# Strassen matmul with tanh: cast blocks of the third column, later stores, another order of transfers

## The chip, the cores and the metric

One core of one Trainium2 chip. The metric is the device time of one launch in microseconds (us), the median of three runs. A profile of one further execution goes with it. The engines are TensorE (PE; its weight loads are shown as PEld), VectorE (DVE), ScalarE (ACT), GpSimd (POOL) and SyncE (SP). Transfers are issued from POOL's queue (in the profile q0, software_dynamic) and from SP's (q1, hardware_dynamic); a transfer that changes the number type is always issued from POOL.

## The reference

```python
m, k, n = 4096, 4096, 4096        # a: (m, k), b: (k, n), bias: (n,), all float32
return np.tanh(np.matmul(a, b) + bias)
```

## The kernel before

The output is made in four columns of 1024 (c = 0 to 3), and in each column in pairs of row blocks, 256 rows each. A pair of one column is one level of Strassen's scheme (Winograd's form) with seven products m1 to m7, in 16-bit floats. `a11` to `a22` are the four quarters of a pair's rows of A, `b11` to `b22` those of the column's B, `s1`, `s2`, `s5`, `s6`, `s7` sums of A's quarters, `d1`, `d3`, `d4`, `e6`, `e7` sums of B's. B's operands stay in SBUF for the column, each in four blocks (`blk` 0 to 3, 512 KB in 16 bits).

The work is a list of 61 **items**, numbered n; the prediction speaks of items by these numbers. An item has a column, one pair, or two pairs for half of the inner dimension. Time is laid out by hand in **slots**, seven for an item; item n has its products at slot 7n + position, and a product of 16 matmuls fills about one slot:

```python
PRODUCTS = {
    0: ("m2", "s2", "b11"),
    2: ("m5", "s5", "b22"),
    4: ("m3", "a11", "d3"),
    5: ("m1", "s1", "d1"),
    6: ("m4", "a22", "d4"),
    8: ("m6", "s6", "e6"),
    10: ("m7", "s7", "e7"),
}
```

So at slot 177 stands m5 of item 25, at 179 m3 of 25, at 182 m2 of 26, at 184 m5 of 26, at 200 m3 of 28. `at_slot(slot, f, ...)` hangs any other work ahead of the products of that slot; each engine takes its instructions in the order in which they are written, and so does each transfer queue.

Items by column: 0 to 12 in column 0, 13 to 28 in column 1, 29 to 44 in column 2, 45 to 60 in column 3. The last two items of a column (11 and 12, 27 and 28, 43 and 44) share two pairs, half of the inner dimension each, and the first two of the next column (13 and 14, 29 and 30, 45 and 46) are the same pairs again with their A still in SBUF: these are the *staying* items, `stays(n)`. Column 1 to 3 have a stretch in which two items at a time go through a second level of the scheme (`four(n)`; items 17 to 24, 33 to 42 and 49 to 60). The last `four` of a column is the *leaving* one.

**Natural items.** In column 0, and for items 26, 27 and 28, A is loaded from the input with a cast (`load_nat`, tile `nat`, rows r = 1 first, then r = 0, in parts u = 0 and 1, four DMAs each, from POOL), transposed on DVE (`turn`, L262) into the quarters, and the quarters are stored to `scratch` in DRAM (`keep`, L292, from SP), because later columns fetch them from there (`fetch`, L296, from SP). `asum` (L148 for all tensor_tensor) writes s2 over a21 and s5 over a12, so what is stored in their place is s2 and s5; later s6 and s7 go over the same tiles. Quarters have two buffers a name, so item n + 2 takes item n's buffer; staying items keep theirs for two items more, and item n + 4 then takes it.

**B of a new column.** `change(c, part, n)` loads B's blocks while the last items of the column before run: for column 2, part 0 (blocks 0 and 1) around item 27 and part 1 (blocks 2 and 3) around item 28: b12 and b21 (`load_raw`) ahead of the others for part 0 and behind them for part 1, b11 at slots 190 (blocks 0, 1) and 197 (blocks 2, 3), b22 at 192 and 199. Each block is four DMAs from the float32 input with a cast, from POOL (L372). The sums d3, e6, d1, d4, e7 follow on DVE from slot 197 on. For column 3, eight blocks are cast earlier, in quarters, into DRAM tiles (`cast_b`, one quarter for each `cast_on`), and then loaded with one DMA a block (L362).

**Leaving.** The second level keeps forms of B in the places of operands (the form t3 of m3, m4, m5 and m7 in one half of d3, d4, b22 and e7). `BACK` says at which step of the leaving `four` which operand is brought back: blocks of b11 and e6, the t3 halves from `away` tiles in DRAM (`move`, L626, from POOL, two DMAs of 256 KB each), the guests (quarters of the next item in other tiles), the loads of the item after next (`nat`), and b12 and b21 of the next column. Step 10 lies ahead of the leaving items' m1, steps 14 to 17 around their m6 and m7.

**After m2.** `after` reads a product's bank with DVE: m2's result is added to the bias, twice, before m5 may write the same bank; m5's result is added before m3 goes on in the bank where that add puts it.

Of the kernel before, what the change touches and what calls it, by code (L numbers as in the profile page):

```python
# [44 lines left out]
SLOTS = 7  # L45
# [22 lines left out]
STAGED = {c: (-8, -6, -4, 1, 4, 7) for c in TWICE}  # L68
ASIDE = {1: (-13, -11, -9, 1, 3, 6), 2: (-13, -11, -9, 1, 3, 6), 3: (-12, -7, -10, -2, 6, 4)}
SAVED = {1: (-7, -5, 8, 10), 2: (-7, -5, 8, 10)}  # L70
SPARED = (0, 1)
S6_AT = 2
AWAY = {"m5": -14, "m7": -3}
# [7 lines left out]

CAST = [(3, blk, *half) for half in ((0, 1), (1, 0), (0, 0), (1, 1)) for blk in range(2)]
CASTING = {1: (-12, -12, -11, -11, 12, 13, 15, 17), 2: (-12, -12, -11, -11, 12, 13, 15, 17)}
CASTING_AT = {"first": (0, 1, 2, 9), "middle": (2, 9)}

# [1 line left out]
BACK = {  # L89
    1: {  # L90
        ("e6", 0): 6, ("e6", 1): 7, ("m7", "t3"): 7, ("b11", 0): 10, ("b11", 1): 10, ("b11", 2): 10, ("b11", 3): 10,
        ("m5", "t3"): 10, ("m3", "t3"): 14, ("m4", "t3"): 15,
        ("guest", "a21"): 8, ("guest", "a12"): 10, ("nat", 1): 11,
    },
# [4 lines left out]
    },  # L99
}  # L100
# [17 lines left out]
def kernel(  # L118
# [7 lines left out]
    nc = tc.nc  # L126
# [250 lines left out]
        load_b(raw[name, blk], c, blk, *((0, 1) if name == "b12" else (1, 0)), nt, queue)  # L377

    def load_op(name, c, blk):
        load_b(new_bop(name, blk), c, blk, *((0, 0) if name == "b11" else (1, 1)))  # L380

    def bsum(name, blk):
        x, y, op = {
# [226 lines left out]
        else:  # L610
            four_right(what, name, rights[what, name], rights.get((what, {"t2": "t1", "t4": "t2"}.get(name))))

    def move(what, c, out_, *names):

        for name, (r, j) in OVER_FOUR.items():
            if names and name not in names:
                continue
            if out_:
                away[what, c, name] = dram.tile([P, TP, NB // 2], fp16, name=f"away_{what}_{c}_{name}")
            for i in range(2):  # L620
                there = away[what, c, name][:, ds(i * TB, TB)]
                here = quarter(what, r, j, i)
                if out_:
                    nc.sync.dma_start(out=there, in_=here)
                else:
                    nc.gpsimd.dma_start(out=here, in_=there)  # L626

    def twice_after(n, what):
        c, (pair,), part, _ = items[n]
# [222 lines left out]
    def give_back(c, step):  # L852
        for (name, part), at in BACK[c].items():
            if at == step:
                if name == "nat":
                    load_nat(ends_with[c] + 1, part)
                elif name == "guest":
                    fetch(ends_with[c], part)
                elif name in TWO:
                    move(name, c, False, part)  # L860
                elif name in ("b12", "b21"):
                    load_raw(name, c + 1, part, nc.sync)
                else:
                    bring_block(name, part)
# [3 lines left out]
    def four(n):  # L868
# [177 lines left out]
        if leave:  # L1046
            take_m5(q)
            take_m1(p)
            if not last:
                fetch(m, "a11", nc.gpsimd if natural(m + 1) else nc.sync)  # L1050
            for name in ("t1", "t2", "t4"):
                del rights["m5", name]
            step(11)
            one_whole("m1", q)
            take_m1(q)
            step(12)
            for i in (p, q):
                one_whole("m6", i)
                step(14 if i == p else 16)
                take_m6(i)  # L1060
                if i == q and natural(m + 1):
                    at_slot(SLOTS * m + 1, one_whole, "m7", q, range(TP))
                    at_slot(SLOTS * m + 3, one_whole, "m7", q, range(TP, T))
                    at_slot(SLOTS * m + 3, take_m7, q)
                    break
                one_whole("m7", i)
                if i == p:
                    for name in ("a21", "a12"):
                        if (m, name) not in guests:
                            fetch(m, name)  # L1070
                    if natural(m + 1):
                        load_nat(m + 1, 0)
                    asum(m, "s2")
                take_m7(i)
                step(15 if i == p else 17)
                if i == p:
                    for name in AHEAD[0]:
                        get(m + 1, name)
            for name in AHEAD[1]:
                get(m + 1, name)  # L1080
            asum(m, "s5")
            for k in range(18, 29):
                at_slot(SLOTS * m + k - 18, give_back, c, k)
            return
# [221 lines left out]
    def prepare(n):  # L1306

        s0 = SLOTS * (n - 1)
        part = items[n][2]
        if again(n):  # L1310
            at_slot(s0, lambda: aset[n].update((i, aset[n - 2][i]) for i in QUADS))
        elif natural(n):
            loads = {0: (-5, -4), 1: (4, 5), 2: (6, 7)}.get(n, (s0 - 7, s0 - 4))
            for r in (1, 0):
                at_slot(loads[1 - r], load_nat, n, r)
                if n == 1 and r:
                    at_slot(loads[0], store_ends, "A")
            turns = {
# [4 lines left out]
            }.get(n, [(i, (s0 + x, s0 + y)) for i, (x, y) in {  # L1323
                "a22": (0, 0), "a21": (2, 2), "a11": (3, 4), "a12": (5, 5)
            }.items()])
            if n - 2 in fours:
                turns = [(i, (x + 1, y + 1)) for i, (x, y) in turns]
            for name, at in turns:
                at_slot(at[0], turn, n, name, 0)
            for name, at in turns:  # L1330
                at_slot(at[1], turn, n, name, 1)
                if n == 0 and name == "a22":
                    at_slot(-1, asum, n, "s2", 0)
                if name in ("a11", "a22"):
                    at_slot({0: {'a22': -1, 'a11': 5}, 1: {'a22': 12, 'a11': 15}, 2: {'a22': 17, 'a11': 18}}.get(n, {}).get(name, at[1]), keep, n, name)
        else:
            behind = n - 2 in partner
            for name, at in (
                ("a22", 1 if behind else 0), ("a21", 1),
                ("a11", -1 if n in second else 0 if behind else 2), ("a12", 4),  # L1340
            ):
                if part == 1 and n - 2 in fours and name != "a12":
                    continue
                if name == "a12" and n - 2 not in twos and n > LEAD + 1 and n - 2 not in fours:
                    early_fetch.add(n)
                elif name != "a12" or n - 2 not in twos:
                    at_slot(s0 + at, fetch, n, name)
        late = stays(n)
        end_ = n == len(items) - 1
        sums_at = {"s2": 4, "s5": 6, "s1": 9}  # L1350
        sums_at["s6"] = 12 if late else 13 if end_ else 10
        sums_at["s7"] = 15 if late else 12 if end_ else 13
        if n == 0:
            at_slot(-1, asum, n, "s2", 1)
            at_slot(-1, keep, n, "a21")
            sums_at = {"s1": 10, "s5": 11, "s6": 12, "s7": 14}
        elif n == 1:
            sums_at = {"s2": 6, "s1": 9, "s5": 9, "s6": 13, "s7": 15}
        elif n == 2:
            sums_at = {"s2": 6, "s1": 8, "s5": 9, "s6": 12, "s7": 14}  # L1360
        elif n == 3:
            sums_at["s2"] = 3
        elif n - 2 in partner:
            sums_at["s2"] = 3
        if natural(n) and n - 2 in fours:
            sums_at["s2"], sums_at["s5"] = 5, 7
        if n - 2 in twos and n not in twos and part is None:
            sums_at["s5"] = 8
        for name, at in sums_at.items():
            at_slot(s0 + at, asum, n, name)  # L1370
            if natural(n) and name in ("s2", "s5"):
                at_slot(s0 + at, keep, n, "a21" if name == "s2" else "a12")
        if n < LEAD:
            at_slot(s0 + 11, lead_add, n)
            if n:
                at_slot(s0 + 4, lead_bias, n)
# [280 lines left out]
    def cast_on():  # L1657
        next(casts, None)

    for c in FOURS:  # L1660
        begin_four(c)
        for at in CASTING.get(c, ()):
# [73 lines left out]
```

## Time and profile before

| | |
|---|---|
| median of the runs | 1517.2 us (1516.11, 1517.95, 1517.2) |
| the profiled execution's own time | 1521.58 us |
| its span, first to last instruction | 1519.8 us |
| granted TensorE clock, mean | 0.996 |
| TensorE busy | 1500.8 us, 9461 matmuls |
| DVE, ACT, POOL busy | 1214.8, 403.1, 532.2 us |
| transfers | 410.37 MB, 270 GB/s over the span |

In a timeline a row has start, duration, engine, line, operation, output and inputs by the program's names with buffer numbers left out, shape, how many were merged, and in brackets the engine's idle time before it with what ended it. In a list of waits a row has who waited for whom, us in total, times, the longest. In the chain of waits a row has start, duration and what the chain spent it on; for a transfer that is from issue to landing. `b<-in_b_dram` is a load of B with a cast, `nat<-in_a_dram` one of A, `d<-away_m_t` a t3 half brought back, `a<-scratch` a fetch of a stored quarter, `scratch<-a` a store of one.

### The profile page before, as it was taken

To read this page: it belongs to the slowest core of one execution; us is meant where nothing else is said; L and a number is where in the kernel's file an instruction comes from. 1 tells how busy PE (TensorE), PEld (TensorE's weight loads), DVE (VectorE), ACT (ScalarE), POOL (GpSimd) and SP (SyncE) were. 2 spreads that over 40 slices of the span, in tenths; PEclk is the share of its full clock that TensorE was granted. 3 is DMA by queue.
4 is the path that set the end of the run, shared out by engine and by line. 5 is a ranking of instruction groups with operands and counts; after the bars stand their busy time and mean duration, and the time that the engine had idled before them with its cause. 6 is when DMAs were issued, how large, how long until landed. Compare 5 with 4: busy or idle time off the path is not lost.

```text
span 1519.8 us, 24963 instructions
## 1 busy us (share of the span) xinstructions
PE 1500.8 (99%) x9461; PEld 927.0 (61%) x9461; DVE 1214.8 (80%) x1718; ACT 403.1 (27%) x909; POOL 532.2 (35%) x930
## 2 busy tenths in 40 slices
PE   9999999999999999999989999999999999999999
PEld 4444444444445788864434578888744458888887
DVE  6788977777787888868768788898748869888888
ACT  3341111111222233321112123333213222333332
POOL 8775453334613111155573311121425121111112
PEclk9999999999999999999999999999999999999999
DMA  9999999999999889999999979998999687888895
GB/s 184 173 239 268 293 258 247 215 215 229 218 267 273 267 316 331 342 299 250 247 203 290 273 253 329 340 324 297 312 303 215 214 262 272 308 309 307 320 346 190
DMA packets 206652, 410.37 MB, mean 270 GB/s; under 512 B 26050, under 2 KB 98242, under 8 KB 206532
## 3 DMA queue, kind: packets, MB, share of 16 engines
q0 software_dynamic: 125456, 221.57, 59.8%
q1 hardware_dynamic: 80404, 186.81, 35.1%
q8 instruction: 74, 1.21, 0.3%
q10 hardware_dynamic: 672, 0.39, 0.1%
q14 instruction: 46, 0.38, 0.1%
HBM read 349.70 MB, written 136.31 MB: 320 GB/s over the span
## 4 chain that ended last, share of the span: by engine, by line
PE 89%; DMA 8%; POOL 1%; issue 1%; DVE 1%; ACT 0%; SPq 0%; DVEq 0%; POOLq 0%; ACTq 0%
PE ps L469 39%; PE ps L764 37%; PE ps L828 7%; PE ps L1414 5%; DMA nat<-in_a_dram 4%; DMA d<-away_m_t 1%; DMA b<-in_b_dram 1%; DMA a<-scratch 1%; DMA b<-corner_b 1%; DMA side<-in_b_dram 1%; POOL nat L234 0%; POOL nat L225 0%; DVE a L262 0%; DMA coarse<-in_a_dram 0%; POOL b L372 0%
## 5 line engine op out<-in xcount | busy, mean ns | idle before, releaser
L469 PEld LDWEIGHTS <-a 128*128 128x128 f16 x2592 | 254.5, 98 | 321.2 <-issue 18.8
L764 PEld LDWEIGHTS <-h 128*128 128x128 f16 x2944 | 288.0, 98 | 35.8
L700 POOL DMA_DIRECT2D form<-form_m x196 | 103.9, 530 | 536.5 <-PE ps L764 484.3
L764 PEld LDWEIGHTS <-a 128*128 128x128 f16 x2208 | 216.0, 98 | 33.7 <-issue 0.6
L469 PE MATMUL ps<-b,a 128*128 128x512 f16 x868 | 198.3, 379 | 1.5 <-DVE s L148 1.5
L469 PE MATMUL ps<-d,a 128*128 128x512 f16 x800 | 185.0, 385 | 9.7 <-DVE ps L148 9.7
L262 DVE STREAM_TRANSPOSE a<-nat 128x1024 f16<-128x1024 f16 (+3 forms) x178 | 156.2, 919 | 25.2 <-PE ps L469 13.1
L469 PE MATMUL ps<-e,a 128*128 128x512 f16 x700 | 159.2, 379 | 0.0
L372 POOL DMA_DIRECT2D b<-in_b_dram x224 | 120.8, 545 | 92.3 <-PE ps L469 31.8
L148 DVE TENSOR_TENSOR a<-a,a 128x2048 f16<-128x2048 f16 (+1 forms) x123 | 148.3, 1206 | 0.2
L764 PE MATMUL ps<-form,h 128*128 128x256 f16 x1136 | 144.8, 273 | 0.0
L148 DVE TENSOR_TENSOR h<-a,h 128x1024 f16<-128x1024 f16 x184 | 125.1, 687 | 16.7 <-PE ps L764 16.6
L469 PEld LDWEIGHTS <-s 128*128 128x128 f16 x688 | 67.3, 98 | 79.9
L469 PE MATMUL ps<-d,s 128*128 128x512 f16 x496 | 112.1, 379 | 0.0
L764 PE MATMUL ps<-form,a 128*128 128x256 f16 x896 | 111.5, 273 | 0.1
L828 PE MATMUL ps<-d,a 128*128 128x512 f16 x480 | 108.2, 379 | 0.0
L234 POOL DMA_DIRECT2D nat<-in_a_dram x144 | 76.4, 533 | 88.9 <-DMA nat<-in_a_dram 41.1
L850 ACT CAST ps<-zeros 128x256 f32<-128x256 f16 x192 | 68.7, 380 | 128.4 <-DVE s L148 69.0
L828 PEld LDWEIGHTS <-a 128*128 128x128 f16 x608 | 59.5, 98 | 65.8
L148 DVE TENSOR_TENSOR ds<-ds,ps 128x512 f32<-128x512 f32 (+1 forms) x126 | 83.5, 674 | 9.2 <-PE ps L828 8.3
L148 DVE TENSOR_TENSOR ps<-ps,x 128x256 f32<-128x256 f32 x96 | 41.3, 430 | 46.9 <-PE ps L764 37.2
L494 ACT ACTIVATE o<-ps 128x512 f32<-128x512 f32 x78 | 46.9, 601 | 116.2 <-issue 82.3
(168 smaller groups left out, 1974.3 us busy)
## 6 DMA issues: line engine op xcount, KB each, us to landing
form<-form_m POOLq DMA_DIRECT2D x196, 512.0 KB, 7.2
a<-scratch SPq DMA_DIRECT2D x147, 512.0 KB, 7.4
out_dram<-o SPq DMA_DIRECT2D x186, 256.0 KB, 6.0
nat<-in_a_dram POOLq DMA_DIRECT2D x256, 128.0 KB, 7.1
b<-in_b_dram POOLq DMA_DIRECT2D x192, 128.0 KB, 5.8
scratch<-a SPq DMA_DIRECT2D x48, 512.0 KB, 7.5
form_m<-stage POOLq DMA_DIRECT2D x18, 512.0 KB, 6.2
scratch<-a SPq DMA_DIRECT2D x32, 256.0 KB, 6.2
```

The lines of the kernel that those rows point to most:

```text
L148: nc.vector.tensor_tensor(out=out_, in0=in0, in1=in1, op=op)
L234: nc.gpsimd.dma_start(out=tl[ds(q * QP, QP), :, :], in_=src.rearrange("(mb p) k -> p mb k", p=QP),)
L262: nc.vector.transpose(dst[:, ds(b0 * tb, n * tb), :].rearrange("P (b t) (mb p) -> P mb b t p", t=tb, p=QP), src[:, :, ds(b0, n), :].rearra ...
L372: nc.gpsimd.dma_start(out=dst[ds(q * QP, QP), ds(t, nt)], in_=src)
L469: nc.tensor.matmul(st[where], at, bt, start=(what == "m2" or n < LEAD and what == "m1") and i == 0, stop=i == len(ts_) - 1, skip_group_che ...
L494: nc.scalar.activation(o, src, TANH)
L700: nc.gpsimd.dma_start(out=rights[what, name], in_=forms[what, name])
L764: nc.tensor.matmul(to, at, bt, start=False, stop=t == TP - 1, skip_group_check=True)
L828: nc.tensor.matmul(to[:, half], at[:, t // TB, t % TB], bop[right, t // TB][:, t % TB, half], start=anew and t == 0, stop=t == T - 1, skip ...
L850: nc.scalar.copy(bank(n, 0, where)[:, HALF[half]], zeros)
L1414: nc.tensor.matmul(mb[m % 4, j], aq[m, kt // T][:, kt % T, :], right(kt, j), start=fresh and kt == k0, stop=stop and kt == k1 - 1, skip_gr ...
```

## The change

- Four blocks of column 2's B (b11 and b22, blocks 2 and 3) are cast into DRAM in 16 quarters from POOL, at slots 35, 38, ... 80 in column 0, and later loaded with one DMA a block from SP (`load_op` with a queue) at slots 197 and 199, in the place of 16 DMAs from POOL. The casts for column 3 keep their slots.
- The stores of the staying items 11, 12, 27 and 28 go to slots 7(n + 2) + `LATER`: for item 27 s2 to slot 200, s5 to 202, a22 to 207, a11 to 208, for item 28 s2 to 207, s5 to 209, a22 to 213, a11 to 214. Before, they stood at 182 to 195. Each is two DMAs of 256 KB. Items 11 and 12 move likewise, from 70 to 83 into 88 to 102.
- Leaving column 1: the t3 halves of m3 and m4 come back at steps 10 and 11 in the place of 14 and 15, that of m3 ahead of the loads of item 26's r = 1, that of m4 behind them. The fetch of item 25's a11 goes from POOL to SP.
- Leaving column 2: the same halves come back at steps 16 and 17, from SP in the place of POOL.
- Item 26's transposes stand at slots 178 (a22), 179 (a21), 180 (a11) and 181 (a12) in the place of 176, 178, 179 to 180 and 181.

```diff
+LATER = (4, -3, 5, -1), (3, -3, 4, -1)
...
-CAST = [(3, blk, *half) for half in ((0, 1), (1, 0), (0, 0), (1, 1)) for blk in range(2)]
+CAST = [(2, blk, i, i) for i in range(2) for blk in (2, 3)]
+CAST += [(3, blk, *half) for half in ((0, 1), (1, 0), (0, 0), (1, 1)) for blk in range(2)]
+AHEAD_OF = [SLOTS * 5 + 3 * i for i in range(16)]
...
 BACK = {
     1: {
...
-        ("m5", "t3"): 10, ("m3", "t3"): 14, ("m4", "t3"): 15,
-        ("guest", "a21"): 8, ("guest", "a12"): 10, ("nat", 1): 11,
+        ("m5", "t3"): 10, ("m3", "t3"): 10,
+        ("guest", "a21"): 8, ("guest", "a12"): 10, ("nat", 1): 11, ("m4", "t3"): 11,
     },
     2: {
...
-        ("m5", "t3"): 10, ("m3", "t3"): 14, ("m4", "t3"): 15,
+        ("m5", "t3"): 10, ("m3", "t3"): 16, ("m4", "t3"): 17,
...
     def load_op(name, c, blk):
-        load_b(new_bop(name, blk), c, blk, *((0, 0) if name == "b11" else (1, 1)))
+        queue = nc.sync if c == 2 else nc.gpsimd
+        load_b(new_bop(name, blk), c, blk, *((0, 0) if name == "b11" else (1, 1)), queue=queue)
...
-    def move(what, c, out_, *names):
+    def move(what, c, out_, *names, queue=nc.gpsimd):
...
-                if out_:
-                    nc.sync.dma_start(out=there, in_=here)
-                else:
-                    nc.gpsimd.dma_start(out=here, in_=there)
+                (nc.sync if out_ else queue).dma_start(*(there, here) if out_ else (here, there))
...
                 elif name in TWO:
-                    move(name, c, False, part)
+                    move(name, c, False, part, queue=nc.gpsimd if step < 12 else nc.sync)
...
             if not last:
-                fetch(m, "a11", nc.gpsimd if natural(m + 1) else nc.sync)
+                fetch(m, "a11")
...
             if n - 2 in fours:
-                turns = [(i, (x + 1, y + 1)) for i, (x, y) in turns]
+                turns = [("a22", (3, 3)), ("a21", (4, 4)), ("a11", (5, 5)), ("a12", (6, 6))]
+                turns = [(i, (s0 + x, s0 + y)) for i, (x, y) in turns]
...
-                if name in ("a11", "a22"):
+                if name in ("a11", "a22") and not stays(n):
...
-            if natural(n) and name in ("s2", "s5"):
+            if natural(n) and name in ("s2", "s5") and not stays(n):
                 at_slot(s0 + at, keep, n, "a21" if name == "s2" else "a12")
+        if natural(n) and stays(n):
+            for at, name in zip(LATER[part], ("a22", "a21", "a11", "a12")):
+                at_slot(SLOTS * (n + 2) + at, keep, n, name)
...
+    for at in AHEAD_OF:
+        at_slot(at, cast_on)
     for c in FOURS:
         begin_four(c)
```

## The prediction

> **What bounds the kernel now.** I read the totals first, then what TensorE waits for, then its timeline around each wait, then DVE, the chain of waits and the DMA queues there.
>
> ```profile
> PE 1500.8 (99%) x9461; PEld 927.0 (61%) x9461; DVE 1214.8 (80%) x1718; ACT 403.1 (27%) x909; POOL 532.2 (35%) x930
> PE ps L469 <- DVE ps L148: 9.7, 4, 6.0
> PE ps L469 <- DMA a<-scratch: 2.3, 1, 2.3
> PE ps L469 <- DVE s L148: 1.5, 2, 0.8
> ```
>
> TensorE is busy 1500.8 of the 1519.8 us span. The change touches no matmul, so it can only win or lose idle time, and time in which the clock is lowered after an idle gap. The three rows hold 13.5 us; where they lie is in TensorE's timeline (start, duration, idle before).
>
> ```profile
> 684.65 3.62 PE L469 MATMUL ps<-b,a 128*128 128x512 f16 x16
> 688.10 1.89 PE L828 MATMUL ps<-e,a 128*128 128x512 f16 x8
> 692.40 5.30 PE L469 MATMUL ps<-d,a 128*128 128x512 f16 x16 [2.41 <-DVE ps L148]
> 697.53 3.62 PE L469 MATMUL ps<-d,s 128*128 128x512 f16 x16
> 712.31 3.61 PE L469 MATMUL ps<-b,a 128*128 128x512 f16 x16 [0.80 <-DVE s L148]
> 764.11 3.62 PE L469 MATMUL ps<-e,s 128*128 128x512 f16 x16
> 773.68 6.08 PE L469 MATMUL ps<-d,a 128*128 128x512 f16 x16 [5.95 <-DVE ps L148]
> 1110.88 1.04 PE L469 MATMUL ps<-side,a 128*128 128x512 f16 x4 [2.33 <-DMA a<-scratch]
> ```
>
> A product (16 matmuls) takes 3.45 us from start to start. Three places matter. **A**, item 25 to item 26: 2.41 idle before m3 of 25, which then runs 5.30 instead of 3.62 (1.68 lost to the clock), then 0.80 before m5 of 26. **B**, item 28, before m3: 5.95 idle and 6.08 - 3.62 = 2.46 of clock, together 8.4. **C**, item 43, m2: 2.33, and no clock loss. The other idle gaps lie before 170 us, where nothing is changed.
>
> What was late at A and B is in DVE's timeline, and the loads behind it in the chain of waits (start, duration, what):
>
> ```profile
> 686.48 1.25 DVE L262 STREAM_TRANSPOSE a<-nat 128x1024 f16<-128x1024 f16 x1 [2.00 <-DMA nat<-in_a_dram]
> 689.38 1.25 DVE L262 STREAM_TRANSPOSE a<-nat 128x1024 f16<-128x1024 f16 x1 [1.65 <-DMA nat<-in_a_dram]
> 691.65 0.69 DVE L148 TENSOR_TENSOR ps<-ps,s 128x512 f32<-128x512 f32 x1
> 768.38 1.23 DVE L148 TENSOR_TENSOR d<-b,b 128x2048 f16<-128x2048 f16 x1 [8.49 <-DMA b<-in_b_dram]
> 771.79 1.22 DVE L148 TENSOR_TENSOR d<-b,b 128x2048 f16<-128x2048 f16 x1
> ```
>
> ```profile
> 684.03 6.39 DMA d<-away_m_t
> 700.73 9.03 DMA nat<-in_a_dram
> 709.84 1.25 DVE a L262
> 711.67 0.59 DVE s L148
> 764.60 5.98 DMA b<-in_b_dram
> 1100.04 10.80 DMA a<-scratch
> ```
>
> So at A the a22 transposes of item 26 wait for their loads and hold back, in DVE's order, the add that m3 needs (691.65). At B two sums d3 wait for b22. At C the fetch of item 43's a21 took 10.80. All three are late transfers. How full the DMA engines are between 706 and 754 (queue: packets, MB, share of 16 engines; then an issue row: KB each, us to landing):
>
> ```profile
> q0 software_dynamic: 5952, 5.31, 72.8%
> q1 hardware_dynamic: 3274, 6.38, 38.3%
> scratch<-a SPq DMA_DIRECT2D x16, 256.0 KB, 6.2
> ```
>
> The shares sum to 111%: full. SP's queue moved 6.38 MB in 0.383 x 48 = 18.4 us of all engines, 0.76 us for 256 KB.
>
> **Part by part. B, the later stores.** The 16 scratch rows are the stores of the staying items 27 and 28. All move behind slot 200, where m3 of 28 begins, so 16 x 0.76 = 12.1 us of engine time leaves the stretch in which b22 is still queued. Two of the four B blocks now on SP (b11, 2 x 512 KB) become loadable when m2 of 28 ends, about 757, and compete: 4 x 0.76 = 3.0 back. b22's blocks 0 and 1 stay on POOL, ahead of the removed loads, so leaving POOL's queue does not help them. Net they land about 9 us sooner, less the 1 to 2 us that A costs below. Needed: the first d sum 5.95 sooner, and the second b22 block (landed 764.60 + 5.98 = 770.58) by 765.8, when the second sum must start, 4.7 sooner. Both hold, and B goes: -8.4. Bounds: -8.4, and -3.7 if b22 comes only 3 us sooner (2.95 idle and 1.7 of clock left).
>
> Behind the two waits that SP gains (b11 for m2 of 28, b22 for m5 of 28) are the column's bias row and the late stores; no output is due before m3 of 28 ends. Price 0; above it, an output is late by what a load is late, and outputs have no reader.
>
> **A, transposes later, queue order.** With a22 moved from slot 176 to 178, the add follows m5 of 25 (684.65 + 3.45) at once, and m3 can start at 690.0. It also needs d3's t3 half, which landed only at 684.03 + 6.39 = 690.4 and, for its second issue, later. That pair of DMAs moves ahead of item 26's loads (step 10), m4's to step 11, and the fetch of a11 goes to SP, so this does not bind again. Products m3, m1, m4, m2 and m6 would then end at 690.0 + 5 x 3.45 = 707.3. But m5 of 26 needs m2's result read out of its bank, and these two adds stand on DVE behind item 27's a22 transposes, whose last load landed at 700.73 + 9.03 = 709.76; 709.84 to 712.26 are the transpose and the adds, and m5 began at 712.31. Nothing is taken off the engines before that landing: a11's 512 KB only changes queue, both t3 pairs are ahead of it before and after. So A's idle time moves to m5 of 26 and stays. It may grow, since TensorE's head start brings these stores (SP's timeline) up to 4 us forward, into the same stretch:
>
> ```profile
> 697.13 0.33 SPq L484 DMA_DIRECT2D out_dram<-ds  x1
> 698.89 0.33 SPq L484 DMA_DIRECT2D out_dram<-o  x1
> 705.75 0.34 SPq L484 DMA_DIRECT2D out_dram<-o  x1
> ```
>
> At 0.76 each, between 0 and 2.3; I take 1.2. Then one gap of 712.3 + 1.2 - 707.3 = 6.2 us, part of it perhaps already before m2 of 26 (its s2 is behind a11's transposes). The 1.68 of clock that the profile paid at m3 was spent inside this wait; now it falls after the wait and counts. I take 1.7, the lower of the two observed; bounds 0 (as at 1110.88) and 2.5. A: +2.9, from -5.0 (712.3 - 707.3, all of it gone) to +4.8.
>
> The clock rows say that 2.41 us idle can halve the rate (5.30 against 3.62) and that 2.33 need not. [...]
>
> **C, t3 loads of column 2.** Rows of 1095 to 1112, then POOL's and SP's timelines:
>
> ```profile
> d<-away_m_t POOLq DMA_DIRECT2D x4, 256.0 KB, 8.5
> 1098.06 0.75 POOL L626 DMA_DIRECT2D d<-away_m_t  x1 [0.28 <-DMA b<-form_m]
> 1104.85 0.34 SPq L484 DMA_DIRECT2D out_dram<-ds  x1
> ```
>
> These four, 3.0 us of engine time issued from 1098.06 on, share the engines with the a21 fetch (1100.04 + 10.80) and now come after it, from SP at steps 16 and 17. The fetch gains 3.0 at most and needs 2.33. m3's pair is then issued behind the 1104.85 store; with 8.5 to landing it is there by 1114, and m3 of 43 starts at 1108.55 + 6.9 = 1115.5; with 10.8 it would be 0.7 late. I take -2.0, bounds -2.3 and +0.7.
>
> **Column 0 and its end.** The 16 quarter casts (4 blocks x 4, exactly the 16 slots 35 to 80) have DVE's and POOL's waits of 170 to 470 us and the price of a cast as rows:
>
> ```profile
> DVE a L262 <- PE ps L469: 11.7, 16, 1.0
> POOL nat L234 <- DVE a L262: 32.4, 8, 10.2
> L372 POOL DMA_DIRECT2D cast<-in_b_dram x32: 518/567/821, 413.4 to 998.8; - x32
> ```
>
> No transpose waits there for a load; POOL waits up to 10.2 us for a buffer that DVE still reads, so the loads are ahead. 16 x 0.57 = 9.1 us of POOL's time over 165 us is covered: 0; without that cover a late transpose would cost its lateness. At the column's end the same 16 stores of items 11 and 12 move from slots 70 to 83 into 88 to 102, where DVE runs without a gap and TensorE follows it closely:
>
> ```profile
> 441.50 1.29 DVE L148 TENSOR_TENSOR ps<-ps,s 128x512 f32<-128x512 f32 x2
> 442.65 3.62 PE L469 MATMUL ps<-d,a 128*128 128x512 f16 x16
> ```
>
> The first of the two adds ends at about 442.2 for a product at 442.65. Slower output stores can hold DVE's output buffers: +0.3, bounds 0 and +2.
>
> **Sum.** -8.4 - 2.0 + 2.9 + 0.3 = -7.2, made on the profiled run (1521.58 us, span 1519.8), 4.4 us above the median of 1517.2; part of that may be the clock terms, which a run has or not. I take the whole difference to the median: **1510.0**. With A from 0 to +4.8 and C from -2.3 to +0.7 the forecast's own range is 1506.8 to 1514.6.
>
> **Rivals.**
> - *A's wait disappears.* If item 27's load lands 5 us sooner, A gives -5.0 instead of +2.9: 1502.1. For: POOL's queue loses the a11 transfer ahead of it. Against: engines at 111%. [...] Chance 0.14.
> - *The B blocks take what the stores gave.* b22 then lands only 3 us sooner, B gives -3.7: 1514.7. For: four 512 KB loads start at 757 and 764, just when b22 lands. Chance 0.10.
> - *Slower: the late stores hold up the next column's fetch.* The last a11 store of 12 and 28 now goes out two slots before SP fetches item 16's and 32's a11 into the same buffer, and the fetch must wait for it; all of SP's queue stands behind. Rows of SP and DVE:
>
> ```profile
> 824.68 0.33 SPq L296 DMA_DIRECT2D a<-scratch  x1
> 829.71 0.63 SPq L296 DMA_DIRECT2D a<-scratch  x1
> 842.19 0.68 DVE L148 TENSOR_TENSOR h<-a 128x1024 f16<-128x1024 f16 x1
> ```
>
> The store goes right behind 824.68. With 6.2 to landing (its row above) the fetch moves by about 2 us and is there by 840, before the h at 842.19. With 10.8 for both, the fetch is issued at 836.4 and lands at 847.2, 5.0 late, in both transitions, with 1.7 of clock each: 13.4, so 1523.4. It decides once store and fetch together take over 17 us. Chance 0.07.
> - *The end of column 0 turns DVE-bound:* 2.0 and 1.7 of clock instead of 0.3: 1513.4. Chance 0.06.
>
> **How the numbers follow.** Forecast 0.58, rivals 0.37, none of these 0.05. A measurement of this kernel tells about 0.2% (3 us) from no change, so faster means below 1514.2. Forecast (but for 0.02), the first rival and nearly all of the last are faster: 0.80 and a share of the rest, 0.81; same 0.10, mostly the second rival; slower 0.09. The range 1503 to 1517 leaves out the best of the first rival and the slower cases.
>
> **What would show it.** Right: TensorE's 5.95 wait and the one at 1110.88 are gone; m3 of 25 follows without idle, and a wait on DVE of 4 to 6 us stands before m5 of 26, in front of it a transpose waiting for nat. Wrong: that wait is under 1 us (first rival), d<-b,b still waits on b<-in_b_dram over 3 us with TensorE idle behind it (second), or h<-a waits for a<-scratch beside a new TensorE gap at the start of columns 1 and 2 (third).

## The result, and the profile after

The changed kernel takes 1510.3 us, median of six runs (1507.4 to 1512.9); the kernel before took 1516.7 on the same chip (1514.4 to 1519.3). The ratio is 0.9958, 95% interval 0.9943 to 0.9973: 6.4 us faster (4.1 to 8.6). The profiled run took 1510.32 us, its span is 1508.6.

The totals, and then what TensorE waits for (engine, tile, line, releaser: us in total, times, longest). Line numbers have moved: 473 is the product that was 469, 151 VectorE's arithmetic that was 148.

```profile
PE 1495.9 (99%) x9461; PEld 925.3 (61%) x9461; DVE 1214.4 (80%) x1718; ACT 402.9 (27%) x909; POOL 528.4 (35%) x925
PE ps L473 <- DVE s L151: 4.2, 2, 3.5
PE ps L473 <- DVE ps L151: 2.2, 2, 1.8
PE ps L473 <- DVE a L151: 0.4, 1, 0.4
```

The wait of 2.3 us for a<-scratch has left the list, and the longest wait is 3.5 us where it was 6.0; the two waits that make up the 2.2 lie before 170 us. TensorE's timeline at the three places (start, duration, what, idle before):

```profile
683.63 3.62 PE L473 MATMUL ps<-b,a 128*128 128x512 f16 x16
688.81 3.62 PE L473 MATMUL ps<-d,a 128*128 128x512 f16 x16
699.75 1.04 PE L473 MATMUL ps<-side,a 128*128 128x512 f16 x4 [0.42 <-DVE a L151]
710.33 5.30 PE L473 MATMUL ps<-b,a 128*128 128x512 f16 x16 [3.50 <-DVE s L151]
763.81 3.62 PE L473 MATMUL ps<-e,s 128*128 128x512 f16 x16
767.27 3.62 PE L473 MATMUL ps<-d,a 128*128 128x512 f16 x16
1099.50 1.03 PE L473 MATMUL ps<-side,a 128*128 128x512 f16 x4
```

At A, m3 of 25 (688.81) follows without idle, and the idle time stands before m5 of 26: 3.50 us, and 5.30 - 3.62 = 1.68 of clock behind it (over the 7 us from 709 to 716 the granted clock is 0.76; from 690 to 697 it is 1.00). At B, m3 of 28 (767.27) starts 3.46 after the product ahead of it, as if nothing had ever been late. At C, m2 of 43 (1099.50) has no wait. What stood behind these, on VectorE, and then on SyncE's queue and GpSimd:

```profile
707.86 1.25 DVE L265 STREAM_TRANSPOSE a<-nat 128x1024 f16<-128x1024 f16 x1 [1.73 <-DMA nat<-in_a_dram]
709.60 0.67 DVE L151 TENSOR_TENSOR s<-ps,bias_bc 128x512 f32<-128x512 f32 x1
759.52 1.22 DVE L151 TENSOR_TENSOR d<-b,b 128x2048 f16<-128x2048 f16 x1
762.92 1.22 DVE L151 TENSOR_TENSOR d<-b,b 128x2048 f16<-128x2048 f16 x1
```

```profile
756.24 8.09 SPq L365 DMA_DIRECT2D b<-cast  x4
764.85 1.25 SPq L295 DMA_DIRECT2D scratch<-a  x2
757.29 4.28 POOL L375 DMA_DIRECT2D b<-in_b_dram  x8 [6.30 <-DVE s L151]
```

The two sums d3 (759.52, 762.92) wait for no load any more. GpSimd issued the last quarter of b22 at 750.44, and it landed 5.6 later, at 756.1, just ahead of SyncE's loads (756.24). GpSimd then stands 6.30 us until a buffer is free for the next load. The queues between 706 and 754:

```profile
q0 software_dynamic: 8045, 7.21, 100.5%
q1 hardware_dynamic: 1175, 2.39, 14.2%
```

SyncE's queue moves 2.39 MB there instead of 6.38, and GpSimd's 7.21 instead of 5.31: the engines are as full as before (114.7% for the two queues against 111.1%), and the room that the stores left is taken by the loads that were late.

The spans differ by 11.2 us, the medians by 6.4. The profiled run of before was 4.9 us above its median, and 1.1 us of the difference arose before 170 us, where nothing was changed.

### The profile page after: what moved, and what is told of

The parts are those of the page before. It is cut to its first block, busy times and chain, and to the rows that moved or that the text cites. A ratio compares the mean times of both kernels' runs of the same rounds, so it can differ in the third digit from the quotient of the medians.

```text
span 1508.6 us, 24955 instructions
## 1 busy us (share of the span) xinstructions
PE 1495.9 (99%) x9461; PEld 925.3 (61%) x9461; DVE 1214.4 (80%) x1718; ACT 402.9 (27%) x909; POOL 528.4 (35%) x925
## 4 chain that ended last, share of the span: by engine, by line
PE 90%; DMA 6%; POOL 1%; issue 1%; DVE 1%; ACT 0%; POOLq 0%; DVEq 0%
PE ps L473 41%; PE ps L765 37%; PE ps L829 7%; PE ps L1419 5%; DMA nat<-in_a_dram 4%; DMA d<-away_m_t 1%; DMA out_dram<-o 1%; DMA e<-form_m 0%; DVE a L265 0%; DMA side<-in_b_dram 0%; POOL nat L228 0%; POOL nat L237 0%; POOL out_dram L1557 0%; ACT o L1552 0%; DVE a L151 0%
## 5 line engine op out<-in xcount | busy, mean ns | idle before, releaser
L473 PE MATMUL ps<-d,a 128*128 128x512 f16 x800 | 180.8, 379 | 2.2 <-DVE ps L151 2.2
L375 POOL DMA_DIRECT2D b<-in_b_dram x208 | 112.0, 546 | 87.7 <-PE ps L473 32.0
L829 PE MATMUL ps<-d,a 128*128 128x512 f16 x480 | 108.2, 379 | 0.0
```

The costliest lines, as they stand in the source:

```text
L375: nc.gpsimd.dma_start(out=dst[ds(q * QP, QP), ds(t, nt)], in_=src)
L473: nc.tensor.matmul(st[where], at, bt, start=(what == "m2" or n < LEAD and what == "m1") and i == 0, stop=i == len(ts_) - 1, skip_group_che ...
L829: nc.tensor.matmul(to[:, half], at[:, t // TB, t % TB], bop[right, t // TB][:, t % TB, half], start=anew and t == 0, stop=t == T - 1, skip ...
```

## The experiments

All ratios are against the kernel before on the same chip, with 95% intervals. 0.001 is 1.5 us. They fall into three groups: each part alone or taken back, the casts' queue, and the order on VectorE at A.

**The stores taken back.** In the changed kernel:

```diff
-                if name in ("a11", "a22") and not stays(n):
+                if name in ("a11", "a22"):
-            if natural(n) and name in ("s2", "s5") and not stays(n):
+            if natural(n) and name in ("s2", "s5"):
-        if natural(n) and stays(n):
-            for at, name in zip(LATER[part], ("a22", "a21", "a11", "a12")):
-                at_slot(SLOTS * (n + 2) + at, keep, n, name)
```

> The changed kernel with the sixteen scratch stores of the staying items (11, 12, 27, 28) back at their old slots; casts, queues and the order at the leaving pairs stay as changed. Theory (the stores alone made the wait before m3 of 28): b22's second block lands again at about 770 us of the span, TensorE waits again 5 to 6 us before m3 of 28 and may lose 2 us of clock behind it, the wait of 3.5 us before m5 of 26 stays: 1510.3 + 6 to 8 = 1516 to 1518 us. Rival 1 (the four cast blocks on SyncE's queue did it): b22 lands by 760, no wait there, 1510 to 1511 us. Rival 2 (the new order at items 24 to 26 did it): the same, 1510 to 1511 us.

Measured: 1519.1 us, ratio 1.0005 (0.9995 to 1.0014). All of the gain is gone, against rivals 1 and 2; the time is 1 us above the theory's range. TensorE and VectorE, and the last b22 quarter in the chain of waits:

```profile
774.38 5.78 PE L473 MATMUL ps<-d,a 128*128 128x512 f16 x16 [7.23 <-DVE ps L151]
772.49 1.22 DVE L151 TENSOR_TENSOR d<-b,b 128x2048 f16<-128x2048 f16 x1 [3.65 <-DMA b<-in_b_dram]
760.69 11.77 DMA b<-in_b_dram
```

B is back and worse than in the kernel before: 7.23 instead of 5.95. That b22 quarter was issued sooner than in the kernel before (760.69 against 764.60) and landed later, after 11.77 us instead of 5.98.

**The stores alone.** The same edit the other way round, in the kernel before.

> The kernel before with nothing but the sixteen scratch stores moved to the later slots. Theory (stores): b22's second block lands at 756 to 760 us of the span, no wait before m3 of 28; the waits before m3 of 25 (2.4) and before m2 of 43 (2.3) stay as in the kernel before: 1516.7 - 6 to 8.4 = 1508 to 1511 us. Rivals 1 and 2 (casts, order): the wait of about 6 us before m3 of 28 stays, 1516 to 1517 us. If the gain is between, 1511 to 1515 us, the parts share it.

Measured: 1512.5 us, ratio 0.9964 (0.9951 to 0.9976), so 5.5 us faster (3.6 to 7.4). B is gone (m3 of 28 at 767.26 has no idle time ahead of it), A and C stay, and there is a new wait. TensorE, VectorE, ScalarE and SyncE's queue, at A (the rows of 683.66 and 709.54, used further below), at B and at the start of column 2, and the DMA queues of 795 to 832:

```profile
683.66 3.62 PE L470 MATMUL ps<-b,a 128*128 128x512 f16 x16
767.26 3.62 PE L470 MATMUL ps<-d,a 128*128 128x512 f16 x16
834.63 3.61 PE L470 MATMUL ps<-b,a 128*128 128x512 f16 x16 [1.59 <-DVE s L149]
709.54 1.25 DVE L263 STREAM_TRANSPOSE a<-nat 128x1024 f16<-128x1024 f16 x1 [3.22 <-DMA nat<-in_a_dram]
833.29 0.70 DVE L149 TENSOR_TENSOR ps<-ps,bias_bc 128x512 f32<-128x512 f32 x1 [5.81 <-ACT o L495]
832.66 1.25 ACT L495 ACTIVATE o<-ps 128x512 f32<-128x512 f32 x2 [5.90 <-DMA out_dram<-o]
818.58 4.71 SPq L297 DMA_DIRECT2D a<-scratch  x1
826.51 1.30 SPq L485 DMA_DIRECT2D out_dram<-o  x2
q0 software_dynamic: 2435, 4.09, 40.9%
scratch<-a SPq DMA_DIRECT2D x12, 256.0 KB, 9.0
```

ScalarE stands 5.90 us for an output buffer, because the output stores are issued only at 826.51: in SyncE's queue they stand behind scratch stores, t3 halves and a fetch that held the queue 4.71 us, and the scratch stores take 9.0 us to land. VectorE's adds wait for ScalarE, and TensorE for them. In the changed kernel the same step and the same queues read:

```profile
820.00 2.51 SPq L488 DMA_DIRECT2D out_dram<-o  x2
827.10 0.60 ACT L498 ACTIVATE o<-ps 128x512 f32<-128x512 f32 x1 [0.35 <-DMA out_dram<-o]
q0 software_dynamic: 826, 2.61, 18.8%
scratch<-a SPq DMA_DIRECT2D x12, 256.0 KB, 4.2
```

So the late stores do cost the next column, by way of the output buffers, unless something takes load off the engines there (the two queues of 795 to 832 make 105.1% in the run with the stores alone, 96.5% in the changed kernel): the wait stands in all three profiles with late stores and without the casts (1.59 here, 1.16 and 1.63 in two runs below) and in none with both.

**Half of the stores.** The kernel before with `LATER` for item 27 only:

```diff
-        if natural(n) and stays(n):
+        if natural(n) and n == 27:
```

> The kernel before with only the eight stores of item 27 moved to the later slots, half of the sixteen of column 1. Theory (the lateness of b22 is the engine time of the stores ahead of it): b22's second block, which landed at 770.6 in the kernel before and at 760.6 with all of them late, lands in the middle, 764 to 767, so the wait of 6 us before m3 of 28 falls to 0 to 2 us: ratio 0.996 to 0.998. Rival (the wait goes with all sixteen or not at all, by an order in a queue): still 5 to 6 us of wait, ratio 0.999 to 1.0.

Measured: 1513.8 us, ratio 0.9972 (0.9961 to 0.9984).

```profile
762.29 1.23 DVE L149 TENSOR_TENSOR d<-b,b 128x2048 f16<-128x2048 f16 x1 [3.00 <-DMA b<-in_b_dram]
767.58 3.61 PE L470 MATMUL ps<-d,a 128*128 128x512 f16 x16 [0.46 <-DVE ps L149]
```

Eight stores instead of sixteen leave a first sum that still waits 3.00 us for b22 (8.49 before, none with all sixteen) and 0.46 us on TensorE. In the traces the last b22 quarter lands at 770.6 in the kernel before, at 764.9 here, and at 760.6 with all sixteen late. So the lateness goes down in steps with the stores taken away, as engine time would have it; the rival, an order in a queue, had expected 5 to 6 us of wait still. Over all the runs of this document, that quarter lands between 756.1 and 761.8 in the seven profiles with all stores of items 27 and 28 late, and between 767.2 and 772.6 in the six with none.

**Column 1's stores alone late.** The changed kernel with items 11 and 12 at their old slots (`and n > 12` in the condition above).

> The changed kernel with the eight stores of items 11 and 12 (end of column 0) back at their old slots; those of items 27 and 28 stay late. Theory (the gain is made by the stores of 27 and 28; in column 0 no wait was there to remove): no change against the changed kernel, ratio about 0.996, 1510 to 1511.5 us where the kernel before stands at 1517. Rival: the late stores at the end of column 0 cost something through the output buffers (VectorE waited 2.5 instead of 2.2 us there): 1 to 2 us faster.

Measured: 1509.2 us, ratio 0.9951 (0.9939 to 0.9963), beside 0.9958 (0.9943 to 0.9973) for the changed kernel. The gain is made by items 27 and 28. Whether the stores at the end of column 0 cost 1 us is inside the intervals.

**The casts alone, over SyncE's queue.** The kernel before with `CAST`, `AHEAD_OF` and the queue of `load_op` as in the change.

> The kernel before with nothing but the four blocks of column 2's B cast in column 0 and loaded over SyncE's queue. Theory (stores): b22's first two blocks are on GpSimd's queue ahead of the removed loads, they land at about 770 us, the wait of about 6 us before m3 of 28 stays, and the sixteen casts in column 0 cost nothing: 1515.5 to 1517.5 us. Rival 1 (casts): b22 lands by 762, the wait is under 1 us, 1508 to 1511 us. Third possibility: the casts cost what column 0 pays for them, 1518 us or more, with new waits for transposes between 200 and 400 us.

Measured: 1521.1 us, ratio 1.0021 (1.0012 to 1.003), slower by 3.2 us (1.8 to 4.6). The third possibility named the size, but not the place: no new wait in column 0. TensorE, SyncE's queue, and the last b22 quarter in the chain of waits:

```profile
774.53 5.41 PE L472 MATMUL ps<-d,a 128*128 128x512 f16 x16 [8.32 <-DVE ps L150]
755.02 8.09 SPq L364 DMA_DIRECT2D b<-cast  x4
763.77 8.80 DMA b<-in_b_dram
```

B has grown from 5.95 to 8.32. SyncE's four loads of 512 KB start at 755.02, when b22 is still being loaded over GpSimd's queue. The first two of them land at 761.1 and 763.3, while b22's last quarter takes 8.80 and lands at 772.6.

**The same casts, loaded over GpSimd's queue.**

```diff
-        queue = nc.sync if c == 2 else nc.gpsimd
+        queue = nc.gpsimd
```

> The kernel before with the four blocks cast in column 0, as in the run with the casts alone, but loaded over GpSimd's queue instead of SyncE's. Theory (the casts alone cost 3 us because SyncE's loads of b11 overtake b22's last quarters, which took 9 to 12 us to land instead of 6): on GpSimd's queue they stand behind b22, the wait before m3 of 28 is 6 us again, ratio 0.999 to 1.001. Rival (the casting itself costs column 0 the 3 us): ratio 1.002 as over SyncE's queue.

Measured: 1516.4 us, ratio 0.999 (0.9979 to 1.0002), 4.7 us less than over SyncE's queue, the intervals apart. Casting and loading together cost nothing. Nor does the casting alone: between 170 and 680 us GpSimd is busy 187.0 us here and 177.8 in the kernel before, close to the 9.1 more that the prediction priced, and TensorE is busy over 509.9 of the 510 in both. The wait before m3 of 28 is not 6 but 2.37 us in this profile; that part of the expectation failed, and one profile can't say by what.

```profile
769.36 3.61 PE L472 MATMUL ps<-d,a 128*128 128x512 f16 x16 [2.37 <-DVE ps L150]
```

**The change without the casts.** `CAST`, `AHEAD_OF` and the queue of `load_op` as before, the rest as changed.

> The changed kernel without the four cast blocks (they load over GpSimd's queue as before); stores, column 1's and column 2's order as changed. Theory (the casts are worth nothing to the wait before m3 of 28 once the stores are late): b22's second block lands by 762, no wait there, 1509.5 to 1511 us. Rival: the casts are worth 2 us or more, through SyncE's queue or the output buffers at the start of column 2 (there the stores alone left a gap of 1.6 us at 834.6): 1512 us or more. Third possibility: the sixteen casts cost column 0 what they showed alone, about 3 us, also here: 1507 us.

Measured: 1511.6 us, ratio 0.9962 (0.9949 to 0.9976): the same as with them. B is gone here too, and the wait of the stores-alone run is there again, so the casts take it away, but the medians don't resolve what that is worth:

```profile
832.11 3.61 PE L470 MATMUL ps<-b,a 128*128 128x512 f16 x16 [1.63 <-DVE s L149]
```

**Column 1's order alone.** `BACK[1]`, the queue of a11 and item 26's turns as changed, in the kernel before.

> The kernel before with nothing but the new order at the end of column 1's fours (t3 loads of m3 and m4 earlier, a11 of item 25 over SyncE, item 26's transposes two slots later). Theory as predicted: the 2.4 us before m3 of 25 are gone, a wait of 3 to 6 us stands before m5 of 26, the wait of about 6 us before m3 of 28 stays: 1516.7 + 0 to 3 = 1516.5 to 1519.7 us. Theory as the trace of the changed kernel has it (item 27's last load 0.9 us earlier against item 25, not 1.2 later): +0.7, 1517.4 us. Rival 2 (this order also brings b22 sooner): the wait before m3 of 28 under 2 us, 1509 to 1512 us.

Measured: 1516.8 us, ratio 0.9991 (0.9982 to 1.0), between nothing and 2.7 us faster; the 2.9 us predicted as A's loss are excluded.

```profile
683.52 3.62 PE L469 MATMUL ps<-b,a 128*128 128x512 f16 x16
700.88 1.04 PE L469 MATMUL ps<-side,a 128*128 128x512 f16 x4 [1.65 <-DVE a L148]
710.12 3.61 PE L469 MATMUL ps<-b,a 128*128 128x512 f16 x16 [2.16 <-DVE s L148]
707.65 1.25 DVE L262 STREAM_TRANSPOSE a<-nat 128x1024 f16<-128x1024 f16 x1 [0.40 <-DMA nat<-in_a_dram]
```

The idle time does move from m3 of 25 to m2 and m5 of 26, but it gets shorter, and m5 runs at full clock (3.61). Item 27's last a22 transpose starts 707.65 - 683.52 = 24.13 us after m5 of 25; in the kernel before that was 709.84 - 684.65 = 25.19. In the five profiles with the new order and item 27's transposes in their place it is 24.03 to 24.51, in five of the six with the old order 24.94 to 25.88; the sixth is the next run.

**Column 2's order alone.** `BACK[2]` and the queue of `move` as changed, in the kernel before.

> The kernel before with nothing but the t3 loads of column 2's m3 and m4 issued later and over SyncE's queue. Theory: the fetch of item 43's a21 lands 2 to 3 us sooner, TensorE's wait of 2.3 us before m2 of 43 falls under 0.4, nothing new before m3 of 43; the waits before m3 of 25 and of 28 stay: 2.0 to 2.7 under the kernel before, 1514 to 1515 us where that stands at 1516.7 (2.7 is what is left of the whole change when the parts run so far are taken away). Rival (the fetch is slow because the engines are full there whichever queue loads): the 2.3 us stay, no change. Second rival: m3 of 43 now waits for its t3 half, 0.5 to 2 us slower.

Measured: 1516.8 us, ratio 0.9992 (0.9983 to 1.0). TensorE's list has no wait at m2 of 43 and none at m3. The expected 2.0 to 2.7 us lie in and just above the upper part of the interval (0 to 2.6). This profile also shows no wait before m5 of 26 (0.80 before) and 3.11 instead of 2.41 before m3 of 25, so the places where nothing was changed vary by as much. Item 27's last a22 transpose, too, started only 707.24 - 684.45 = 22.79 us after m5 of 25 here. For C the other traces help: all six with column 2's old order have the wait for `a<-scratch` before m2 of 43 (1.35 to 2.37 us), none of the eight with the new one has it.

**VectorE's order at A.** The changed kernel with one transpose moved: item 27's second a22 turn goes behind the two adds that read item 26's m2.

```diff
-                "a22": (0, 0), "a21": (2, 2), "a11": (3, 4), "a12": (5, 5)
+                "a22": (0, 1 * (n - 3 in fours)), "a21": (2, 2), "a11": (3, 4), "a12": (5, 5)
```

> The changed kernel with one instruction moved: of item 27's two a22 transposes the second, which waits for the last load, goes behind the two adds of item 26's m2 on VectorE. Theory (m5 of 26 waits only because these adds stand behind that transpose in VectorE's order): TensorE's wait of 3.5 us before m5 of 26 falls to about 0.5 and the 1.7 us of clock behind it go: 1510.3 - 4 to 5 = 1505.5 to 1506.5 us. Rival (VectorE is the bound there, the wait moves on): the next add, of item 26's m5, comes late instead, 2 to 3.5 us of TensorE's idle time before m3 of 26, 1508 to 1510.5 us.

Measured: 1505.7 us, ratio 0.9922 (0.991 to 0.9933), below the changed kernel's interval. VectorE and TensorE:

```profile
706.60 0.67 DVE L151 TENSOR_TENSOR ps<-ps,bias_bc 128x512 f32<-128x512 f32 x1
707.18 0.67 DVE L151 TENSOR_TENSOR s<-ps,bias_bc 128x512 f32<-128x512 f32 x1
707.78 1.23 DVE L265 STREAM_TRANSPOSE a<-nat 128x1024 f16<-128x1024 f16 x1
700.31 1.04 PE L473 MATMUL ps<-side,a 128*128 128x512 f16 x4 [1.12 <-DVE a L151]
707.91 3.61 PE L473 MATMUL ps<-b,a 128*128 128x512 f16 x16 [0.52 <-DVE s L151]
711.36 3.62 PE L473 MATMUL ps<-e,a 128*128 128x512 f16 x16
```

The adds start 2.4 us sooner, m5 of 26 waits 0.52 instead of 3.50 and runs at full clock, and the products behind it follow without idle. The transpose itself starts at 707.78, as in the changed kernel (707.86): nothing was done about the load, only the adds no longer stand behind it.

**Both transposes moved.** `"a22": (n - 3 in fours,) * 2`.

> The changed kernel with both of item 27's a22 transposes behind the two adds of item 26's m2. Theory: no wait before m5 of 26, 1505 to 1506 us. Rival: the transposes, the difference for s1 and the a12 transposes now push the add of item 26's m5 back, 1 to 3 us idle before m3 of 26, 1507 to 1510.5 us.

Measured: 1506.1 us, ratio 0.992 (0.9908 to 0.9932), as with one. The wait before m5 is gone altogether, and 1.0 us stands before m3 of 28 instead; neither is resolved. With TensorE ahead, SyncE's loads start at 750.82, before the last b22 quarter is issued (753.13), and that quarter takes 7.97 to land; with one transpose moved it takes 8.16, and 0.39 us stands there.

**And s2 moved up.** The kernel with one transpose moved, and item 26's s2 at slot 4 instead of 5, ahead of the a11 transposes.

> The changed kernel with the second a22 transpose of item 27 behind the two adds of item 26's m2 (1505.7 us, ratio 0.992) and, besides, item 26's s2 ahead of its a11 transposes on VectorE. Theory: the 1.1 us before m2 of 26, which wait for s2 behind the a11 transposes, go: 1504 to 1505 us, ratio 0.991 to 0.992. Rival: the wait moves on to m5 of 26, whose adds wait for item 27's first a22 transpose: no change, 1505.5 to 1506 us.

Measured: 1507.4 us, ratio 0.9933 (0.9921 to 0.9945): no gain. The 1.12 before m2 of 26 are gone, and no wait stands before m5, where the rival had put it. 1.02 stand before m3 of 26, behind the transpose that in this profile waits 2.74 us for its load:

```profile
710.55 1.25 DVE L265 STREAM_TRANSPOSE a<-nat 128x1024 f16<-128x1024 f16 x1 [2.74 <-DMA nat<-in_a_dram]
715.95 3.63 PE L473 MATMUL ps<-d,a 128*128 128x512 f16 x16 [1.02 <-DVE ps L151]
```

The fastest version is thus the change with one or both transposes moved: 11 to 12 us under the kernel before.

## Why the prediction was right, and where it was not

The time was forecast as 1510.0 and came out at 1510.3. The main cause, B, and C were right. One step, A, was wrong in its sign, and that the sum fits to 0.3 us is luck: by the runs of the parts alone B was 2.9 us too big, A 4.3 too high and C 0.8 too big, and the errors made up for each other.

- **B, right in cause and step.** The sixteen stores were the cause: with them back the gain is zero, alone they bring 5.5 us, half of them leave half of the lateness. The price by engine time was somewhat high: 16 x 0.76 = 12.1 us, where the stores alone bring the last b22 quarter 770.6 - 760.6 = 10.0 sooner, and half of them 5.7; the forecast needed 4.7. The term was too big for the median: -8.4 is the profiled run, which was 4.9 us above its median, and the stores alone, which take out B and leave A's and C's waits, give -5.5, after the 1.6 paid back at 834.63.
- **The 3.0 us given back by the b11 loads on SyncE: real, but not in the changed kernel's profile.** There b22 has landed (756.1) before SyncE issues them (756.24); in the version with both transposes moved they come first again. Without the late stores they overtake b22, and the run is 3.2 us slower. So the two parts are not additive: the casts lose 3.2 alone, and no loss shows when the stores are late. What the queue changes is which loads go ahead of which: 4.7 us between the same casts on SyncE's and on GpSimd's queue, so the choice of queue is not without a price.
- **A, the step that failed.** The wait moved to m5 of 26 as said, with the transpose that waits for nat in front of it, but it is 3.50 us, not the 4 to 6 named. The clock term came as taken (1.68) in this profile; with the waits of 2.16, 2.52 and 2.80 there of three other runs with this order nothing was lost, so it is a matter of the run. "Nothing is taken off the engines before that landing", and so +1.2, was wrong: the transpose started 707.86 - 683.63 = 24.23 us after m5 of 25, not 25.19 or later. Column 1's order does that by itself (24.13 in its run), the stores alone don't (709.54 - 683.66 = 25.88). The 22.79 of the column 2 run shows that the load can land sooner for other reasons too, so the size is less certain than the direction. In the profiles A costs 26.70 - 27.66 = -1.0 to the start of m5 of 26 and +1.68 of clock, +0.7 instead of +2.9; the run of that part alone, whose profile pays no clock there, is 1.4 us faster (0 to 2.7), not slower. Whether a11's fetch off GpSimd's queue or the earlier t3 loads bring the 1 us was not separated.
- **C, right in cause.** The wait of 2.33 is gone, in this profile and in all eight with the new order, and m3 of 43 doesn't wait. The time of that part alone, -1.2 us (-2.6 to 0), has the 2.0 inside its interval, and nearly nothing as well.
- **Column 0's casts at nothing: right,** shown by the casts on GpSimd's queue (0.999, and no idle time of TensorE between 170 and 680 us). **The end of column 0, +0.3:** not resolved.
- **Sum.** By parts alone: -5.5 (stores), -1.4 (column 1), -1.2 (column 2), +3.2 (casts) make -4.9; together they are -6.4 (-8.6 to -4.1). The casts' +3.2 is not there in the whole, since without them the change gives -5.8 (-7.7 to -3.6). The parts but for the casts add up to -8.1; whether the 2.3 between the two is more than the width of the intervals stays open.
- **The rivals.** A's wait disappears: no, but one instruction's place on VectorE was all that kept it, and moving it gave the 5 us that the rival had looked for in the loads (0.9958 to 0.9922). The B blocks take what the stores gave: not in the changed kernel; with the stores at their old slots this is what happens. The late stores hold up the next column: it has a place and a size, 1.6 us at 834.63, but over output buffers and not over the a11 fetch, and only without the casts, with which the changed kernel takes GpSimd's share of 795 to 832 from 40.9% to 18.8%. The end of column 0: no.

## What to carry to other kernels

When the DMA engines are full (here 111% for the two queues), look for transfers that nobody needs soon among those ahead of a late load: moving them later gave their engine time to the load here, step by step (eight stores brought it 5.7 us sooner, sixteen 10.0). Here the stores were on SyncE's queue and the load on GpSimd's. Putting other loads on a free queue can do the reverse, as the casts alone did when they overtook the late one (3.2 us slower), so test the two parts apart and together. And where an engine waits in order for a load, read what stands behind the waiting instruction before working on the load: here two adds of 0.67 us behind one transpose cost as much as most of the change had gained (moving the transpose took the ratio from 0.9958 to 0.9922).

## What the runs showed of the hardware that was not expected

Whether an idle gap of TensorE costs clock behind it is decided, in these profiles, by more than its length. All gaps of 3.50 us and over did (3.50, 3.79, 4.88, 5.95, 6.21, 7.23, 8.32: the next product took 5.25 to 6.08 instead of 3.62). Of those between 2 and 3.2 us some did and some did not, at the same place in the program: 2.97 before m5 of 26 lost 1.68 (casts over GpSimd's queue), 2.81, 2.53 and 2.16 there lost nothing; 2.41 before m3 of 25 lost 1.68, 3.11 there nothing.

```profile
709.89 5.30 PE L472 MATMUL ps<-b,a 128*128 128x512 f16 x16 [2.97 <-DVE s L150]
692.91 3.61 PE L469 MATMUL ps<-d,a 128*128 128x512 f16 x16 [3.11 <-DVE ps L148]
```

The product behind the 2.97 took 5.30 us, those behind the 2.16 and the 3.11 took 3.61. In the kernel before, the granted clock over the 7 us behind the 2.41 (692 to 699) is 0.76, with 0.50 from 693.5 to 696.5; over the 7 us behind the 2.33 before m2 of 43 (1110 to 1117) it is 1.00.

Whether such losses are behind the spread of the times stays open: the kernel before spreads over 8 us (1513.2 to 1521.6), the version without long gaps over 3 (1505.1 to 1508.2, five runs), but the casts alone, with a gap of 8.32, over only 4 (1519.5 to 1523.1, eleven runs).
